# Group A's query and key projected together for three row blocks, and the first loads regrouped

## The chip, the cores and the metric

The kernel runs on one core of one Trainium2 chip. The number that counts is the device time of one execution in microseconds: the median of three executions of the kernel before is 319.23 us (319.03 to 319.84).

## The reference

One decoder layer in float32 over 256 rows of 1024 values, with two groups of attention heads side by side:

```
xn = RMSNorm(x)
[qA|kA|vA|c_q|c_kv|k_rope] = xn @ W_in      # 512, 512, 512, 768, 256, 32 columns
A: 8 heads of 64, dilated windows (128,1),(512,4),(2048,16), QK-norm, bias by distance
B: 8 heads of latent attention: qb = RMSNorm(c_q) @ W_uq, [k|v] = RMSNorm(c_kv) @ W_ukv,
   shared rotary key, QK-norm, dense causal softmax
h   = x + concat(A, B) @ W_o
out = h + relu(RMSNorm(h) @ W1)^2 @ W2
```

## The kernel before, in words

Every product is made of three matmuls in a fast float32 form: each operand is split into a high part (ACT casts it) and a low part (DVE subtracts), and hi·hi, hi·lo and lo·hi are added up in PSUM (`three`, L267). So every weight block passes through ACT (L216, tile `his`) and DVE (L217, tile `los`) before PE may use it, and so does every activation block (L245 on ACT, L246 on DVE, tile `two`). The weights come as one packed array in chunks in the order of use. SP issues the loads in the order of the program text (L206, three buffers `raw`); split pieces have five buffers.

x arrives transposed and unscaled (`xraw`, eight blocks of 128 rows); `split_scaled` multiplies by the norm's gain, which lies in `cols`, a small tile that ACT's own DMA queue loads (L189). The row's own norm factor is applied later. The projections then follow in the order q of group A, k of group A, the latents `cq0`, `cq1` and `kv`, and `va` (the values of group A). Each accumulates over eight row blocks into two banks of the pool `acc` (four banks), one for each half of the 256 rows. q and k are normed, transposed on PE (L375) and written to `qT_a` and `kT_a`; six units of scores, softmax and transposes (`probs`, `keys_first`) follow for group A. The latents wait in `nats`; `transposed_split` (L249) turns them on PE through a bank of the pool `mm` (two banks) and splits them into `cT`, a tile of the pool `two`. From `cT` the up-projections `uq0`, `uq1`, `ukv0`, `ukv1` start, and from there PE's order is written out by hand (`STEPS`, L111).

Ahead of `STEPS` the framework's scheduler sets the order on each engine: it lists the program with a model of the times and writes one fixed order for each engine. Each engine then works through its own list and waits at an instruction until its operands are there and its output buffer is free.

Of the kernel before, what the change touches and what calls it, by code (L numbers as in the profile page):

```python
# [51 lines left out]
def shape_constants():  # L52
# [9 lines left out]
    for i, d in enumerate(dist):  # L62
        if d >= 0:
# [9 lines left out]

G_MIX, G_FFN, G_C, G_QKA, G_QKB, C_ROPE = 0, 8, 16, 24, 26, 28
C_INV = C_ROPE + 2 * ROPE
# [4 lines left out]
CHUNK = 2048  # L80
SOURCE = {"cq0": "w_in", "cq1": "w_in", "kv": "w_in", "qa": "w_in", "ka": "w_in", "va": "w_in", "uq0": "w_uq",
          "uq1": "w_uq", "ukv0": "w_ukv", "ukv1": "w_ukv", "wo": "w_o", "ff1": "w_ff1", "ff2": "w_ff2"}
CHUNKS = [(f"{z}a", 4 * i, 4, c, 512) for z, c in (("q", 0), ("k", 512)) for i in range(2)]
CHUNKS += [(f"cq{b}", 4 * i, 4, CQ0 + 384 * b, 384) for b in range(2) for i in range(2)]
CHUNKS += [("kv", 4 * i, 4, KV0, KVR + ROPE) for i in range(2)]
CHUNKS += [("va", 4 * i, 4, 1024, 512) for i in range(2)]
CHUNKS += [(f"uq{b}", 4 * i, 4 - 2 * i, 384 * b, 384) for b in range(2) for i in range(2)]
CHUNKS += [(f"ukv{b}", 0, 2, 512 * b, 512) for b in range(2)]
CHUNKS += [("wo", 0, 4, 512 * b, 512) for b in range(2)]
CHUNKS += [("wo", 4 + 2 * i, 2, 512 * b, 512) for i in range(2) for b in range(2)]  # L90
_FF1 = [[("ff1", 4 * i, 4, n * FB, FB) for i in range(2)] for n in range(NFB)]
_FF2 = [[("ff2", 4 * n + 2 * i, 2, 0, DM) for i in range(2)] for n in range(NFB)]
CHUNKS += _FF1[0] + sum([_FF1[n] + _FF2[n - 1] for n in range(1, NFB)], []) + _FF2[NFB - 1]
OFFSETS = [0]
for _c in CHUNKS:
    OFFSETS.append(OFFSETS[-1] + P * _c[2] * _c[4])

PIECE = 1024
PIECES = []
for _i, _c in enumerate(CHUNKS):  # L100
    _step = -(-_c[2] // -(-_c[2] * _c[4] // PIECE))
    PIECES += [(_i, _r, min(_step, _c[2] - _r), _c[4]) for _r in range(0, _c[2], _step)]

# [47 lines left out]
def tile_layer(ctx, tc, x, xt, pos_in, cols_in, rows_in, w_all, out):  # L151
# [42 lines left out]
    queue = {"load": 0, "split": 0, "at": 0, "raw": {}, "parts": {}}  # L194

    def load_next(cuts=(0,)):

        i = queue["load"]
        _, _, a, _, n = CHUNKS[i]
        raw = raws.tile([P, CHUNK], F32, name="raw")[:, :a * n]  # L200
        o = OFFSETS[i]
        src = w_all[o:o + P * a * n].rearrange("(p n) -> p n", p=P)
        queue["raw"][i] = raw.rearrange("p (a n) -> p a n", a=a)
        queue["load"] += 1
        for c0, c1 in zip(cuts, cuts[1:] + (a,)):
            nc.sync.dma_start(out=raw[:, c0 * n:c1 * n], in_=src[:, c0 * n:c1 * n])  # L206
            yield

    def split_next():
        i = queue["split"]  # L210
        c, r, a, n = PIECES[i]
        while queue["load"] <= c:
            list(load_next())
        raw = queue["raw"][c][:, r:r + a, :]
        hi, lo = (p.tile([P, PIECE], F32R, name=p.name)[:, :a * n].rearrange("p (a n) -> p a n", a=a) for p in (his, los))
        A.copy(out=hi, in_=raw)  # L216
        V.tensor_tensor(out=lo, in0=raw, in1=hi.bitcast(F32), op=ALU.subtract)  # L217
        queue["parts"][i] = hi, lo
        queue["split"] += 1
# [21 lines left out]
    def gain(i):  # L241
        return cols[:, i:i + 1]

    def split_scaled(src, g, hi, lo):
        a = A.activation(out=hi, in_=src, func=AF.Copy, scale=g)  # L245
        v = V.scalar_tensor_tensor(out=lo, in0=src, scalar=g, in1=hi.bitcast(F32), op0=ALU.mult, op1=ALU.subtract)  # L246
        return a.ins, v.ins
# [51 lines left out]
    starts = [load_next((0, 1, 2, 3)), load_next((0, 2)), load_next((0, 2))]  # L299
    next(starts[0])  # L300
    for k in range(0, KD, 2):
        nc.sync.dma_start(out=xraw[:, k:k + 2, :], in_=xt[k * P:(k + 2) * P, :].rearrange("(k p) s -> p k s", p=P))
        next(starts[k // 4])
        if k == 0:
            split_next()
        elif k == 2:
            next(starts[0])
        for kk in (k, k + 1):
            split_scaled(xraw[:, kk, :], gain(G_MIX + kk), xT[0][:, kk, :], xT[1][:, kk, :])
            if kk == 2:  # L310
                split_next()
        split_next()
    next(starts[2])
    nc.sync.dma_start(out=rows, in_=rows_in)
    nc.sync.dma_start(out=xs[0], in_=x[0:P, :])
    next(starts[2])
    nc.sync.dma_start(out=xs[1], in_=x[P:2 * P, :])
    nc.sync.dma_start(out=pos_i, in_=pos_in)

# [41 lines left out]

    for name in ("qa", "ka"):
        ps = project(name, xT, 0, KD)
        for t in range(NT):
# [201 lines left out]
    qk_b = tiny(1, "qk_b")  # L566
    V.scalar_tensor_tensor(out=qk_b, in0=gain(G_QKB), scalar=-1.0 / math.sqrt(DB), in1=gain(G_QKB + 1), op0=ALU.mult, op1=ALU.mult)
    s_q = [tiny(NT * 4, f"s_q{b}").rearrange("p (t h) -> p t h", t=NT) for b in range(2)]
# [173 lines left out]
def packed_cols(i):  # L742

    rows = [i[n].reshape(-1, P) for n in ("norm_mix_g", "norm_ffn_g", "cq_norm_g", "ckv_norm_g")]
# [3 lines left out]
    return np.concatenate([np.concatenate(rows).T, np.broadcast_to(wide, (P, wide.size))], axis=1)  # L748


# [4 lines left out]
def packed_weights(i):  # L755

    return np.concatenate([i[w][k0 * P:(k0 + a) * P, c0:c0 + n].reshape(a, P, n).transpose(1, 0, 2).reshape(-1)
                           for w, k0, a, c0, n in ((SOURCE[c[0]], *c[1:]) for c in CHUNKS)])

# [20 lines left out]
```

## Time and profile before

| what | value |
|---|---|
| median of three executions | 319.23 us (319.03 to 319.84) |
| the profiled execution | 320.25 us |
| span of its instructions | 318.5 us |
| PE (matmul) busy | 311.1 us, 98% of the span |
| DVE busy | 216.5 us, 68% |
| ACT busy | 176.5 us, 55% |
| POOL busy | 38.4 us, 12% |
| first matmul of a projection | at 6.49 us |

The profiled execution's own time lies 1.75 us above its span, and 1.02 us above the median of the three others. Busy time says how long an engine had an instruction in it; PE's matmuls overlap, so the distance between the starts of two of them is what counts there, not the duration of one.

### The profile page before, as it was taken

Reading aid. Unit: us, or ns where it says so; the run is one execution under the profiler, and the core shown is the slowest. Engines: PE = TensorE matmul, PEld = TensorE weight load, DVE = VectorE, ACT = ScalarE, POOL = GpSimd, SP = SyncE. Lnnn points to the kernel's source line nnn. Section 1 sums busy time; section 2 is a strip of 40 time slices with the busy share of each in tenths; the row PEclk is TensorE's granted clock in tenths of the full one; section 3 lists DMA queues with packets and bytes.
Section 4 is the critical chain, followed back from the end, with each engine's and each line's share of the span. In section 5 each row is a group of like instructions: output and inputs, shape, how many; then the busy total and the mean of one; then the engine's idle time right before and its main releaser. Section 6 shows DMA issues by size and latency. Waiting matters only on the chain.

```text
span 318.5 us, 4481 instructions
## 1 busy us (share of the span) xinstructions
PE 311.1 (98%) x1642; PEld 266.0 (84%) x1642; DVE 216.5 (68%) x416; ACT 176.5 (55%) x314; POOL 38.4 (12%) x61
## 2 busy tenths in 40 slices
PE   6999999999999999999999999999999999999995
PEld 4878999989987887888888888888888888888883
DVE  3869899964887994647896574764755845846622
ACT  4875558957796584429574454444643644545400
POOL 1026501080368000001000000000000000000000
PEclk9999999999999999999999999999999999999999
DMA  7989554243842174305577456646446365553002
GB/s 215 389 336 324 189 188 197 66 151 75 315 141 66 68 262 134 134 0 206 191 255 273 163 204 182 241 138 224 173 150 245 137 227 182 176 205 132 0 31 103
DMA packets 12294, 56.43 MB, mean 177 GB/s; under 512 B 1480, under 2 KB 3792, under 8 KB 7536
## 3 DMA queue, kind: packets, MB, share of 16 engines
q1 hardware_dynamic: 11072, 55.02, 49.7%
q10 hardware_dynamic: 1200, 1.12, 1.1%
q8 instruction: 13, 0.21, 0.2%
q14 instruction: 9, 0.07, 0.1%
HBM read 55.07 MB, written 1.06 MB: 176 GB/s over the span
## 4 chain that ended last, share of the span: by engine, by line
PE 96%; DMA 1%; ACT 1%; DVE 0%; issue 0%; DVEq 0%; SPq 0%; ACTq 0%
PE acc L144 57%; PE sc L144 20%; PE mm L144 15%; PE mm L147 4%; DMA big<-in_xt_dram 1%; ACT big L576 0%; ACT sqs L359 0%; ACT two L245 0%; ACT nats L596 0%; DVE x L723 0%; DVEq L776 0%; SPq L206 0%; ACT vb L600 0%; ACTq L245 0%
## 5 line engine op out<-in xcount | busy, mean ns | idle before, releaser
L217 DVE TENSOR_TENSOR los<-raw,his 128x1024 fp32r<-128x1024 f32 (+3 forms) x106 | 121.3, 1150 | 68.9 <-ACT his L216 68.7
L216 ACT CAST his<-raw 128x1024 fp32r<-128x1024 f32 (+3 forms) x106 | 104.1, 992 | 89.8 <-PE acc L144 41.9
L144 PE MATMUL acc<-his,two 128*128 128x512 f32 (+2 forms) x320 | 96.3, 375 | 1.5 <-ACT two L245 1.5
L144 PEld LDWEIGHTS acc<-his,two 128*128 128x128 f32 x320 | 59.4, 191 | 9.5 <-ACT two L245 2.3
L144 PE MATMUL acc<-two,his 128*128 128x512 f32 x240 | 63.2, 393 | 0.0
L144 PE MATMUL acc<-los,two 128*128 128x512 f32 (+2 forms) x160 | 59.6, 373 | 0.0
L144 PE MATMUL sc<-his,big 128*128 128x512 f32 x128 | 49.0, 389 | 0.0
L144 PE MATMUL mm<-his,big 128*128 128x512 f32 x128 | 49.0, 389 | 0.0
L144 PEld LDWEIGHTS acc<-two,his 128*128 128x128 f32 x240 | 42.6, 189 | 7.1
L144 PEld LDWEIGHTS acc<-two,los 128*128 128x128 f32 x240 | 34.5, 190 | 3.4
L144 PE MATMUL acc<-two,los 128*128 128x256 f32 x240 | 35.8, 282 | 0.0
L144 PEld LDWEIGHTS acc<-los,two 128*128 128x128 f32 x160 | 30.6, 192 | 3.9 <-issue 0.6
L144 PEld LDWEIGHTS mm<-his,big 128*128 128x128 f32 x128 | 24.0, 188 | 5.1
L144 PEld LDWEIGHTS sc<-his,big 128*128 128x128 f32 x128 | 24.1, 188 | 4.8
L144 PE MATMUL sc<-los,big 128*128 128x512 f32 x64 | 25.0, 390 | 0.0
L144 PE MATMUL mm<-los,big 128*128 128x512 f32 x64 | 24.9, 389 | 0.0
L408 ACT ACTIVATE half<-half,mx 128x128 f32<-128x128 f32 (+1 forms) x32 | 14.2, 445 | 4.4 <-DVE mx L405 4.3
L144 PEld LDWEIGHTS mm<-los,big 128*128 128x128 f32 x64 | 12.0, 188 | 2.5
L694 ACT COPY half<-acc 128x256 f32<-128x256 f32 x30 | 9.7, 372 | 7.8 <-PE acc L144 7.8
L144 PEld LDWEIGHTS sc<-los,big 128*128 128x128 f32 x64 | 12.0, 188 | 2.2
L695 DVE TENSOR_TENSOR half<-acc,half 128x256 f32<-128x256 f32 x30 | 11.3, 416 | 1.3 <-ACT half L694 1.3
L246 DVE SCALAR_TENSOR_TENSOR two<-mm,cols,two 128x256 fp32r<-128x256 f32 x16 | 7.3, 481 | 6.5 <-ACT two L245 6.3
(140 smaller groups left out, 282.9 us busy)
## 6 DMA issues: line engine op xcount, KB each, us to landing
raw<-in_weights_dram SPq DMA_DIRECT2D x37, 1024.0 KB, 4.8
raw<-in_weights_dram SPq DMA_DIRECT2D x10, 512.0 KB, 3.7
raw<-in_weights_dram SPq DMA_DIRECT2D x6, 768.0 KB, 4.3
raw<-in_weights_dram SPq DMA_DIRECT2D x2, 576.0 KB, 4.1
raw<-in_weights_dram SPq DMA_DIRECT2D x4, 256.0 KB, 5.7
big<-in_xt_dram SPq DMA_DIRECT2D x4, 256.0 KB, 5.7
x<-in_x_dram SPq DMA_DIRECT2D x2, 512.0 KB, 8.3
big<-vec_d ACTq DMA_DIRECT2D x1, 1024.0 KB, 6.8
```

The source lines that it names most:

```text
L144: return self._issue(self.tc.nc.tensor.matmul(**kw))
L147: return self._issue(self.tc.nc.tensor.transpose(**kw))
L216: A.copy(out=hi, in_=raw)
L217: V.tensor_tensor(out=lo, in0=raw, in1=hi.bitcast(F32), op=ALU.subtract)
L246: v = V.scalar_tensor_tensor(out=lo, in0=src, scalar=g, in1=hi.bitcast(F32), op0=ALU.mult, op1=ALU.subtract)
L408: A.activation(out=sb[:, i, :], in_=sb[:, i, :], func=AF.Exp, scale=-1.0, bias=mx[:, i:i + 1], accum_out=mx[:, 4 + i:5 + i])
L694: A.copy(out=zs, in_=ps[2 * b + i][:, S:])
L695: V.tensor_tensor(out=zs, in0=ps[2 * b + i][:, 0:S], in1=zs, op=ALU.add)
```

## The change

The weights of q and k of group A become one sequence `qk` of sixteen blocks of 128 rows by 512 columns: for the row blocks 0, 1 and 2 the q block and then the k block, after that q for the blocks 3 to 7 and k for the blocks 3 to 7. Both products accumulate at the same time, in all four banks of `acc`. The transposed x is packed by partition on the host, with the gains of the first norm in front of it; ACT's queue loads the gains and x block 0 in one DMA (`first`), and SP loads block 1 alone and the others in pairs. All loads and splits of this opening are kept in program order. `cols` (without those gains), `rows` and `pos_i` are loaded after the last chunk of `qk`, and the two products of gains `qk_a` and `qk_b` move from DVE (one instruction each) to POOL (two each).

```diff
+TOGETHER = 3
+QK = [(k, z) for k in range(TOGETHER) for z in range(2)] + [(k, z) for z in range(2) for k in range(TOGETHER, KD)]
...
+CHUNKS = [("qk", [(k, 512 * z) for k, z in QK[4 * i:4 * i + 4]], 512) for i in range(4)]
...
+    first = const.tile([P, NMIX + S], F32, name="first")
+    A.dma_start(out=first, in_=xt[:, 0:NMIX + S])
...
-    A.dma_start(out=cols, in_=cols_in)
...
+    def pinned(ins):
+        return tc.keep_in_program_order(ins) if starting else ins
...
+    starts = [load_next(cuts) for cuts in ((0, 1, 2), (0, 2), (0, 2), (0, 2))]
+    for chunk_or_x in (0, (1, 2), 0, 0, (2, 4), 1, (4, 6), 1, (6, 8), 2, 2):
+        if isinstance(chunk_or_x, int):
+            next(starts[chunk_or_x])
+        else:
+            load_x(*chunk_or_x)
+    split_x(0)
+    split_next()
+    split_next()
+    for k in range(1, KD):
+        split_x(k)
+        if k in (1, 2, 4, 6, 7):
             split_next()
+        if k == 1:
+            split_next()
+    load(out=xs[0], in_=x[0:P, :])
+    load(out=xs[1], in_=x[P:2 * P, :])
+    next(starts[3])
+    next(starts[3])
+    load(out=cols, in_=cols_in)
+    load(out=rows, in_=rows_in)
+    load(out=pos_i, in_=pos_in)
+    starting.clear()
...
-    V.scalar_tensor_tensor(out=qk_a, in0=gain(G_QKA), scalar=1.0 / math.sqrt(DA), in1=gain(G_QKA + 1), op0=ALU.mult, op1=ALU.mult)
+    G.tensor_tensor(out=qk_a, in0=gain(G_QKA), in1=gain(G_QKA + 1), op=ALU.mult)
+    G.tensor_scalar(out=qk_a, in0=qk_a, scalar1=1.0 / math.sqrt(DA), scalar2=None, op0=ALU.mult)
...
+    qk_ps = [[bank(acc) for _ in range(NT)] for _ in range(2)]
+    def qk_steps():
+        i = 0
+        while i < len(QK):
+            w = weights("qk")
+            for j in range(w[0].shape[1]):
+                k, z = QK[i]
+                three(qk_ps[z], xT, w, k, j, k == 0, k == KD - 1)
+                i += 1
+                yield k, z
```

The order on the engines moves with it, also far behind the edited lines, since the scheduler writes it anew. On PE, the first matmuls behind the four warming ones; `acc_218` and `acc_219` are q's two banks before:

```order
L144 MATMUL sc_121<-half_102 128x256 x4
L144 MATMUL acc_218<-his_131,two_126 128x512
L144 MATMUL acc_218<-los_132,two_126 128x512
L144 MATMUL acc_219<-his_131,two_126 128x512
L144 MATMUL acc_219<-los_132,two_126 128x512
L144 MATMUL acc_218<-his_131,two_126 128x512
L144 MATMUL acc_219<-his_131,two_126 128x512
```

The same place now; `acc_231` and `acc_232` are q's banks, `acc_233` and `acc_234` k's, `his_144` and `his_148` the high parts of the first q and the first k block:

```order
L155 MATMUL sc_122<-half_102 128x256 x4
L155 MATMUL acc_231<-his_144,two_127 128x512
L155 MATMUL acc_232<-his_144,two_127 128x512
L155 MATMUL acc_233<-his_148,two_127 128x512
L155 MATMUL acc_234<-his_148,two_127 128x512
L155 MATMUL acc_231<-los_145,two_127 128x512
L155 MATMUL acc_231<-his_144,two_127 128x512
```

The first two matmuls are followed by two of k's, which need the second weight block; before, six matmuls stood on the first block alone.

On PE, the end of the value projection and the begin of `uq0`, before; `mm_603` holds the transposes of the latents' blocks 0 and 1, `mm_612` that of block 2, `acc_878` and `acc_879` are the banks of `va`, `acc_963` is the first of `uq0`. Fourteen matmuls of `va` lie between the two groups of transposes:

```order
L147 MATMUL mm_603<-ident_114,nats_521 128x128
L147 MATMUL mm_603<-ident_114,nats_522 128x128
L147 MATMUL mm_603<-ident_114,nats_521 128x128
L147 MATMUL mm_603<-ident_114,nats_522 128x128
L144 MATMUL acc_879<-los_917,two_126 128x512
L144 MATMUL acc_879<-his_916,two_126 128x512
...
L144 MATMUL acc_879<-his_932,two_126 128x512
L144 MATMUL acc_879<-los_933,two_126 128x512
L144 MATMUL acc_879<-his_932,two_126 128x512
L147 MATMUL mm_612<-ident_114,nats_521 128x128
L147 MATMUL mm_612<-ident_114,nats_522 128x128
L144 MATMUL acc_963<-his_967,two_525 128x384
```

The same place now, with `mm_606` and `mm_615` for those transposes, `acc_881` and `acc_882` for `va` and `acc_967` for `uq0`:

```order
L155 MATMUL acc_882<-los_936,two_127 128x512
L155 MATMUL acc_882<-his_935,two_127 128x512
L158 MATMUL mm_606<-ident_115,nats_524 128x128
L158 MATMUL mm_606<-ident_115,nats_525 128x128
L158 MATMUL mm_606<-ident_115,nats_524 128x128
L158 MATMUL mm_606<-ident_115,nats_525 128x128
L158 MATMUL mm_615<-ident_115,nats_524 128x128
L158 MATMUL mm_615<-ident_115,nats_525 128x128
L155 MATMUL acc_967<-his_971,two_528 128x384
L155 MATMUL acc_967<-los_972,two_528 128x384
L155 MATMUL acc_967<-his_971,two_528 128x384
L155 MATMUL acc_968<-his_971,two_528 128x384
```

The four transposes of `mm_606` have moved behind the last matmul of `va`, straight ahead of the products that read their splits.

On ACT in the same place, before; `two_525` is the tile of `cT`, written from the transposes' banks, `va0` and `va1` the results of the value projection:

```order
L245 ACTIVATE two_525<-mm_603,cols_108 128x256
L216 CAST his_1042<-raw_1040 128x768
L245 ACTIVATE two_525<-mm_603,cols_108 128x256
L560 ACTIVATE va0_211<-acc_878,rstd_192 128x512
L560 ACTIVATE va1_212<-acc_879,rstd_192 128x512
L216 CAST his_1058<-raw_1040 128x768
L245 ACTIVATE two_525<-mm_612,cols_108 128x256
L245 ACTIVATE two_525<-mm_693,cols_108 128x256
L216 CAST his_1076<-raw_1074 128x768
```

And now; `two_528` is the tile of `cT`:

```order
L476 COPY pts_399<-mm_500 128x2x256
L239 CAST his_1046<-raw_1044 128x768
L476 COPY pts_399<-mm_518 128x2x256
L610 ACTIVATE va0_223<-acc_881,rstd_204 128x512
L610 ACTIVATE va1_224<-acc_882,rstd_204 128x512
L239 CAST his_1062<-raw_1044 128x768
L268 ACTIVATE two_528<-mm_606,cols_110 128x256
L268 ACTIVATE two_528<-mm_615,cols_110 128x256
L268 ACTIVATE two_528<-mm_606,cols_110 128x256
```

Both splits from the first bank have moved from ahead of `va0` to behind `va0`, `va1` and the cast of a weight piece. DVE's list has the low halves in the same order, behind the low half of that weight piece.

## Rows read from the trace of the kernel before

**Rows 1.** Section 1 of the page: busy time, share of the span, instructions

```profile
PE 311.1 (98%) x1642; PEld 266.0 (84%) x1642; DVE 216.5 (68%) x416; ACT 176.5 (55%) x314; POOL 38.4 (12%) x61
```

**Rows 2.** The waits of PE in the whole span: total, times, longest

```profile
PE acc L144 <- ACT two L245: 1.5, 1, 1.5
...
PE mm L147 <- ACT sqs L359: 0.5, 1, 0.5
```

**Rows 3.** Windows: stretch, length, busy time per engine, clock, DMA share, GB/s

```profile
4.00:6.49 2.49, 0.96 (x4) 0.24 (x2) 0.94 (x4) 1.18 (x3) 0.00 (x0) 1.00 0.98 308
6.49:10.50 4.01, 4.01 (x10) 3.14 (x11) 3.72 (x8) 3.69 (x8) 0.00 (x0) 1.00 1.05 398
31.00:60.00 29.00, 29.00 (x185) 28.28 (x185) 26.49 (x93) 20.15 (x52) 5.88 (x8) 1.00 0.49 172
60.00:90.00 30.00, 30.00 (x173) 27.57 (x172) 21.85 (x48) 21.68 (x46) 11.38 (x21) 1.00 0.51 173
```

**Rows 4.** The first matmuls: start, duration, operation, idle before and releaser

```profile
4.32 0.63 PE L144 MATMUL sc<-half 128*128 128x256 f32 x1
6.49 0.79 PE L144 MATMUL acc<-his,two 128*128 128x512 f32 x1 [1.53 <-ACT two L245]
...
8.36 1.91 PE L144 MATMUL acc<-his,two 128*128 128x512 f32 x4
10.07 0.63 PE L144 MATMUL acc<-los,two 128*128 128x512 f32 x1
```

**Rows 5.** ACT at the start: the first splits

```profile
5.13 0.62 ACT L216 CAST his<-raw 128x512 fp32r<-128x512 f32 x1 [2.46 <-DMA raw<-in_weights_dram]
5.93 0.91 ACT L245 ACTIVATE two<-big,cols 128x256 fp32r<-128x256 f32 x2 [0.18 <-DMA big<-in_xt_dram]
7.00 0.62 ACT L216 CAST his<-raw 128x512 fp32r<-128x512 f32 x1 [0.16 <-DMA raw<-in_weights_dram]
```

**Rows 6.** DMA issues by line: KB each, median us to landing

```profile
raw<-in_weights_dram SPq DMA_DIRECT2D x4, 256.0 KB, 5.7
...
cols<-in_cols_dram ACTq DMA_DIRECT2D x1, 54.0 KB, 4.5
```

**Rows 7.** PE at the end of the value projection

```profile
75.01 0.39 PE L144 MATMUL acc<-los,two 128*128 128x512 f32 x1
75.24 0.39 PE L144 MATMUL acc<-his,two 128*128 128x512 f32 x1
75.47 0.38 PE L147 MATMUL mm<-ident,nats 128*128 128x128 f32 x2
75.61 0.42 PE L144 MATMUL acc<-his,two 128*128 128x384 f32 x1
...
76.04 0.52 PE L144 MATMUL acc<-his,two 128*128 128x384 f32 x2
```

**Rows 8.** ACT in the same stretch

```profile
72.52 0.48 ACT L245 ACTIVATE two<-mm,cols 128x256 fp32r<-128x256 f32 x1
...
74.99 1.38 ACT L560 ACTIVATE va<-acc,rstd 128x512 f32<-128x512 f32 x2 [0.84 <-PE acc L144]
76.25 0.82 ACT L216 CAST his<-raw 128x768 fp32r<-128x768 f32 x1
76.98 0.47 ACT L245 ACTIVATE two<-mm,cols 128x256 fp32r<-128x256 f32 x1
```

**Rows 9.** DVE in the same stretch

```profile
77.11 0.96 DVE L217 TENSOR_TENSOR los<-raw,his 128x768 fp32r<-128x768 f32 x1 [1.95 <-ACT his L216]
77.99 0.87 DVE L246 SCALAR_TENSOR_TENSOR two<-mm,cols,two 128x256 fp32r<-128x256 f32 x2
```

**Rows 10.** Last group A probabilities on DVE, the transposes behind on PE

```profile
66.07 0.61 DVE L411 TENSOR_SCALAR half<-half,mx 128x256 f32<-128x256 f32 x2
...
71.41 0.60 PE L147 MATMUL mm<-ident,half 128*128 128x128 f32 x4
71.84 0.60 PE L147 MATMUL mm<-ident,nats 128*128 128x128 f32 x4
```

More of the change, by code (lines that the diff above doesn't have):

```diff
@@ L80 @@
 CHUNK = 2048
-SOURCE = {"cq0": "w_in", "cq1": "w_in", "kv": "w_in", "qa": "w_in", "ka": "w_in", "va": "w_in", "uq0": "w_uq",
+SOURCE = {"cq0": "w_in", "cq1": "w_in", "kv": "w_in", "qk": "w_in", "va": "w_in", "uq0": "w_uq",
           "uq1": "w_uq", "ukv0": "w_ukv", "ukv1": "w_ukv", "wo": "w_o", "ff1": "w_ff1", "ff2": "w_ff2"}
-CHUNKS = [(f"{z}a", 4 * i, 4, c, 512) for z, c in (("q", 0), ("k", 512)) for i in range(2)]
-CHUNKS += [(f"cq{b}", 4 * i, 4, CQ0 + 384 * b, 384) for b in range(2) for i in range(2)]
@@ L85 @@
[L85 to L91, printed above, removed]
@@ L92, with chunk @@
-_FF2 = [[("ff2", 4 * n + 2 * i, 2, 0, DM) for i in range(2)] for n in range(NFB)]
+TOGETHER = 3
+QK = [(k, z) for k in range(TOGETHER) for z in range(2)] + [(k, z) for z in range(2) for k in range(TOGETHER, KD)]
+def chunk(name, k0, a, c0, n):
+    return name, [(k0 + i, c0) for i in range(a)], n
+CHUNKS = [("qk", [(k, 512 * z) for k, z in QK[4 * i:4 * i + 4]], 512) for i in range(4)]
+CHUNKS += [chunk(f"cq{b}", 4 * i, 4, CQ0 + 384 * b, 384) for b in range(2) for i in range(2)]
+CHUNKS += [chunk("kv", 4 * i, 4, KV0, KVR + ROPE) for i in range(2)]
@@ new lines @@
+CHUNKS += [chunk("va", 4 * i, 4, 1024, 512) for i in range(2)]
+CHUNKS += [chunk(f"uq{b}", 4 * i, 4 - 2 * i, 384 * b, 384) for b in range(2) for i in range(2)]
+CHUNKS += [chunk(f"ukv{b}", 0, 2, 512 * b, 512) for b in range(2)]
+CHUNKS += [chunk("wo", 0, 4, 512 * b, 512) for b in range(2)]
+CHUNKS += [chunk("wo", 4 + 2 * i, 2, 512 * b, 512) for i in range(2) for b in range(2)]
+_FF1 = [[chunk("ff1", 4 * i, 4, n * FB, FB) for i in range(2)] for n in range(NFB)]
+_FF2 = [[chunk("ff2", 4 * n + 2 * i, 2, 0, DM) for i in range(2)] for n in range(NFB)]
@@ L93 @@
 CHUNKS += _FF1[0] + sum([_FF1[n] + _FF2[n - 1] for n in range(1, NFB)], []) + _FF2[NFB - 1]
 OFFSETS = [0]
-for _c in CHUNKS:
-    OFFSETS.append(OFFSETS[-1] + P * _c[2] * _c[4])
+for _, _b, _n in CHUNKS:
+    OFFSETS.append(OFFSETS[-1] + P * len(_b) * _n)
 PIECE = 1024
 PIECES = []
-for _i, _c in enumerate(CHUNKS):
-    _step = -(-_c[2] // -(-_c[2] * _c[4] // PIECE))
-    PIECES += [(_i, _r, min(_step, _c[2] - _r), _c[4]) for _r in range(0, _c[2], _step)]
+for _i, (_, _b, _n) in enumerate(CHUNKS):
+    _a = len(_b)
+    _step = -(-_a // -(-_a * _n // PIECE))
+    PIECES += [(_i, _r, min(_step, _a - _r), _n) for _r in range(0, _a, _step)]
@@ L194, in tile_layer, with load @@
     queue = {"load": 0, "split": 0, "at": 0, "raw": {}, "parts": {}}
+    starting = [True]
+    def pinned(ins):
+        return tc.keep_in_program_order(ins) if starting else ins
+    def load(**kw):
+        pinned(nc.sync.dma_start(**kw))
     def load_next(cuts=(0,)):
         i = queue["load"]
-        _, _, a, _, n = CHUNKS[i]
+        _, blocks, n = CHUNKS[i]
+        a = len(blocks)
         raw = raws.tile([P, CHUNK], F32, name="raw")[:, :a * n]
@@ L205, in load_next @@
         for c0, c1 in zip(cuts, cuts[1:] + (a,)):
-            nc.sync.dma_start(out=raw[:, c0 * n:c1 * n], in_=src[:, c0 * n:c1 * n])
+            load(out=raw[:, c0 * n:c1 * n], in_=src[:, c0 * n:c1 * n])
             yield
@@ L298, in tile_layer, with load_x, split_x @@
     xT = pair()
[L299 to L304, printed above, removed]
-            split_next()
[L306 to L318, printed above, removed]
+    def load_x(k0, k1):
+        load(out=xraw[:, k0:k1, :], in_=xt[:, NMIX + k0 * S:NMIX + k1 * S].rearrange("p (k s) -> p k s", s=S))
+    def split_x(k):
+        src = xraw[:, k, :] if k else first[:, NMIX:]
+        split_scaled(src, first[:, k:k + 1], xT[0][:, k, :], xT[1][:, k, :])
+    starts = [load_next(cuts) for cuts in ((0, 1, 2), (0, 2), (0, 2), (0, 2))]
[10 more added lines that the diff above has]
+        if k in (1, 2, 4, 6, 7):
+            split_next()
+        if k == 1:
[8 more added lines that the diff above has]
+    starting.clear()
     def sumsq(src, dst):
@@ L360, in head_sums @@
         V.tensor_reduce(out=dst, in_=sqv, op=ALU.add, axis=AX.X)
-    for name in ("qa", "ka"):
-        ps = project(name, xT, 0, KD)
+    qk_ps = [[bank(acc) for _ in range(NT)] for _ in range(2)]
[8 more added lines that the diff above has]
+                yield k, z
+    steps = qk_steps()
+    for z, name in enumerate(("qa", "ka")):
+        while next(steps) != (KD - 1, z):
+            pass
+        ps = qk_ps[z]
         for t in range(NT):
@@ L742, in packed_cols @@
 def packed_cols(i):
-    rows = [i[n].reshape(-1, P) for n in ("norm_mix_g", "norm_ffn_g", "cq_norm_g", "ckv_norm_g")]
+    rows = [i[n].reshape(-1, P) for n in ("norm_ffn_g", "cq_norm_g", "ckv_norm_g")]
     rows += [np.tile(i[n], 2)[None] for n in ("qnorm_a_g", "knorm_a_g")]
@@ L755, in packed_weights @@
 def packed_weights(i):
-    return np.concatenate([i[w][k0 * P:(k0 + a) * P, c0:c0 + n].reshape(a, P, n).transpose(1, 0, 2).reshape(-1)
-                           for w, k0, a, c0, n in ((SOURCE[c[0]], *c[1:]) for c in CHUNKS)])
+    return np.concatenate([np.stack([i[SOURCE[name]][k * P:(k + 1) * P, c:c + n] for k, c in blocks], axis=1).reshape(-1)
+                           for name, blocks, n in CHUNKS])
 def kernel(**inputs):
@@ L766 @@
     x = i["x"][0]
-    laid = {"x": x, "xt": x.T, "positions": i["positions"].reshape(NT, P).T, "cols": packed_cols(i),
+    laid = {"x": x, "xt": packed_x(x, i["norm_mix_g"]), "positions": i["positions"].reshape(NT, P).T, "cols": packed_cols(i),
             "rows": packed_rows(i), "weights": packed_weights(i)}
```

16 lines of the change are left out of this document (10 added, 6 removed).

## The prediction

> **What bounds the kernel now.** I read the page's busy shares first: PE has 98% of the span [rows 1], so the question is where PE stands still and whether the change touches that. The list of PE's waits comes next. It holds a wait of 1.5 us for ACT ahead of the first projection and one of 0.5 us much later [rows 2]; nothing else of weight is left. The windows say the same by stretch: from 31 to 60 and from 60 to 90 us PE is busy for all 29.0 and all 30.0 us, while DVE has 26.49 of the 29 [rows 3]. There is next to no stall to win behind the start, and each new wait of PE is paid in full: nothing later has slack to give it back. So only two kinds of places count: the opening, and places where the new order makes PE wait.
>
> The opening costs PE two things. The first projection matmul starts at 6.49, after 1.53 us of idleness behind the warming matmuls [rows 4]. And it runs at half pace: from 8.36 to 10.07 there are four matmuls of 512 columns, 0.427 us each, against 0.23 us from 75.01 to 75.24 [rows 4, 7]; 512 columns in 0.427 us are the 1.2 GHz level, 0.23 us is near the 2.4 GHz one. The windows' clock column reads 1.00 even at 4.00 to 6.49 [rows 3], so here the pace of the matmuls tells the level.
>
> **The opening, part by part.** Before, the start hangs on ACT: the cast of the first weight block begins when it lands (5.13, 0.62 us), then x is split (two blocks in 0.91 us from 5.93), and PE starts 0.1 us after the first of these [rows 4, 5]. Now ACT's queue brings the gains and x block 0 (132 KB) in place of `cols` (54 KB), and SP brings the same first weight block. `cols` took 4.5 us, so it landed at about 5.2 beside the weight block at 5.1 [rows 5, 6]. The extra 78 KB cost 0.25 us at the 308 GB/s of that stretch [rows 3]. Both at 5.35 or so, then x (0.46) and the cast (0.62), then 0.1: start at about 6.5, no gain. The bounds: if x lands first and its split hides in the wait for the weights, the start is 5.13 + 0.62 + 0.1 = 5.85 (0.64 us gained); if `first`, with its 128 separate pieces, takes as long as a block of 256 KB did (5.7 us [rows 6], so 6.4), the start is 7.6 (1.1 us lost). No row shows such a load; I take 6.45, by the nearest row, that of `cols`.
>
> The Trainium skill (DMA: Bandwidth & Descriptors, "Anatomy of one DMA — SWDGE (gpsimd) path") fits a DMA as about 2.0 us plus bytes over 436 GB/s. By it, 388 KB issued at once would be there in 2.9 us. The trace disagrees already before the change: 54 KB took 4.5 us [rows 6], so I give that only a rival's chance.
>
> PE's third matmul now needs the cast of a second weight block. Before, the second block began its cast at 7.00 [rows 5] with about 0.5 MB of loads ahead of it, as now; its cast ends at 7.65. PE comes there at 6.45 + 0.59 + 0.43 = 7.5: a wait of 0.2 us. Further on nothing is short: each row block now brings twelve matmuls, 2.7 us even at full pace, for 640 KB, which take 1.6 us at the 398 GB/s of the windows [rows 3]. The opening sums to +0.15 us.
>
> What else moves there is covered. The two gain products leave DVE (0.15 us each) and become four short operations on POOL, which is 12% busy [rows 1]. `cols`, `rows` and `pos_i` land near 20 us (6.1 MB at that rate behind the first block at 5.1); their first readers on PE and POOL come behind 24 us, when q is complete. Cover gone, PE's bias product would stand in the way until `rows` lands. The later norms of q (complete after 66 matmuls of the pair, not 48 of q alone) have the 30 remaining k matmuls, 6.8 us, as cover, where they had 48; PE waited for none of them before [rows 2].
>
> **The end of the value projection.** Here the order moves against PE. Before, the transposes of latent blocks 0 and 1 stand at 71.84 among the matmuls of `va` [rows 10], and ACT splits block 0 at 72.52, 3 us before `uq0` reads it at 75.61 [rows 7, 8]. Now these transposes come behind the last matmul of `va`, and on ACT the split of block 0 stands behind two evacuations of `va` and a cast of weights, exactly the place that block 2's split has before. So its times can be read off. Call S the start of the last `va` matmul, 75.24 before. ACT evacuates `va` from 74.99 on (1.38 us, bound by the end of the matmuls), casts at 76.25 and splits at 76.98, until 77.45: S + 2.2 [rows 8]. On DVE, the low half of the cast piece runs at 77.11 and the first split's low half from 77.99, done about 78.45: S + 3.2 [rows 9]. PE itself would be ready early: one matmul (0.23) and six transposes (0.6) behind S, at S + 0.85.
>
> - `uq0`'s first matmul waits for the high half until S + 2.25: 1.4 us.
> - Its third needs the low half. It would be due 0.43 us after the first (75.61 to 76.04 [rows 7]), at S + 2.7, and gets it at S + 3.3: 0.6 us.
> - The next transposes need the bank whose second low half comes 0.8 us after the first; the four matmuls between take 0.7: under 0.1 us.
>
> That is 2.05 us. Cross-check: `uq0`'s third matmul stands at 76.04 before; four transposes (0.43, from 71.41 to 71.84 [rows 10]) now come after S, so S lies at 74.8 and the third matmul at 78.1, 2.06 later. The lower bound is the wait for the high half alone, 1.4 us, if DVE is not held by the weight piece; the upper 2.3, if the first evacuation starts late. The later orders on PE and ACT are again those of before, so the delay stays.
>
> **The sum.** +0.15 + 2.05 = +2.2 us. From the profiled execution, 320.25 us (318.5 of span and 1.75 around it), that is 322.45; the profiled execution lies 1.02 above the median of 319.23, and from the median it is **321.4 us**.
>
> **Rivals.**
> - *The new order doesn't bind* (about 319.3, no change): the splits would have to reach PE in time. For it: before, no such wait shows in the same region. Against: the split cannot begin before its transposes end, and those stand behind `va`; only ACT's list could be quicker than its rows. 0.12.
> - *The early loads win* (faster): if 388 KB land by 3.6 us, x and the cast are done at 4.7, and PE goes on when its last warming matmul ends at 4.95 [rows 4], 1.54 us sooner. Without the pause the rise to full pace could come before the projection has run 4.0 us at half of it; that stretch costs 4.0 x (1 - 0.227/0.427) = 1.9 us. Together up to 3.4, minus 2.05: 317.9. It decides from a start before about 5.0. This is the outcome of the fit above. 0.06.
> - *The new wait drops the clock* (slower still): the wait of 1.4 us is nearly as long as the pause of 1.53, after which PE ran at half pace [rows 4]. Another half-paced stretch of 4.0 us adds 1.9: 323.3. The Trainium skill (TensorE: Matmul & The Clock Gate, "The HAM clock gate") says that idleness brings the half rate back. Against: before that pause the clock had not risen, so no row shows a fall. 0.07.
> - *The softmax comes late on DVE* (slower): the rotary tables start later, and some 1.5 us of their small operations now fall among group A's probabilities, where DVE has 26.49 of 29 us [rows 3]. The last probabilities were ready at 66.68, their transposes due at 71.41 [rows 10]: 4.7 us of room. Against: three times the 1.5. If an earlier unit with less room is 1.2 us late: 322.6. 0.09.
>
> **How the numbers follow.** The forecast has 0.66. About what a measurement can tell here from no change is 0.3%, 0.96 us; the forecast's own range, 1.4 - 0.6 to 2.3 + 1.1 us over the median, is 320.0 to 322.6, so nearly all of it is slower: 0.64, with the clock and softmax rivals 0.80. No change gets 0.02 + 0.10 + 0.01 = 0.13; faster 0.02 + 0.05 = 0.07. The range reaches down past the rival without change, to 319.1, and up to 322.8: under it lie half of that rival and the early loads (0.12), above it the fallen clock and a little more (0.08).
>
> **What would show it.** Right: one wait of PE for the ACT split of the latents of about 1.4 us near 75, another of 0.6 us for DVE's low half within 1 us of it, and the first matmul between 6.2 and 6.8 with a wait of some 0.2 us at the third. Wrong: no wait near 75; a first matmul before 5.5 or after 7; matmuls of 0.63 us behind the new wait; or waits of PE between 30 and 72 us for probabilities.

## The result, and the profile after

| what | before | after |
|---|---|---|
| median of the four executions timed side by side | 319.53 us (319.03 to 319.84) | 323.21 us (321.92 to 323.63) |
| ratio, with its 95% interval | | 1.0102 (1.0080 to 1.0124) |
| the profiled execution, and its span | 320.25 us, 318.5 us | 323.22 us, 321.4 us |
| mean granted clock of TensorE in it | 0.999 | 0.994 |

The changed kernel is slower: by 3.7 us between these medians, where the forecast was 2.2. The 323.21 lies 0.4 us above the range's upper end; the ratio, applied to the earlier median, gives 319.23 x 1.0102 = 322.5, which lies inside. A second set of twelve executions (the fifth experiment) gave 322.26 us and 1.0074 (1.0049 to 1.0100): their spread, 319.88 to 323.73, is itself part of the answer.

The busy times of the page say little, as before [rows 1]: PE has 2.5 us more, in the same 1642 instructions.

```profile
PE 313.6 (98%) x1642; PEld 267.4 (83%) x1642; DVE 215.5 (67%) x414; ACT 176.5 (55%) x314; POOL 39.5 (12%) x65
```

The waits of PE (total, times, longest) tell more. The opening's 1.5 us for `two` [rows 2] has become 0.5 us for a weight cast; two new waits stand beside the old one of half a microsecond.

```profile
PE acc L155 <- ACT two L268: 1.2, 1, 1.2
...
PE mm L158 <- ACT sqs L393: 0.6, 1, 0.6
PE acc L155 <- ACT his L239: 0.5, 1, 0.5
PE acc L155 <- DVE two L269: 0.4, 1, 0.4
```

The windows of [rows 3] again: from 31 to 60 PE is still busy throughout; from 60 to 90 it lacks 1.6 us, and the clock column, 1.00 before, reads 0.94.

```profile
31.00:60.00 29.00, 29.00 (x189) 28.59 (x188) 27.54 (x97) 20.42 (x50) 5.99 (x9) 1.00 0.62 211
60.00:90.00 30.00, 28.39 (x150) 25.32 (x150) 19.06 (x46) 19.36 (x43) 8.79 (x21) 0.94 0.46 149
```

**The opening.** On ACT (start, duration, operation, idle before), x block 0 is split at 4.36, so `first`, issued at 0.72, landed within 3.6 us, and the first weight block was there when that split ended: its cast starts at 4.77, without a wait, against 5.13 before [rows 5].

```profile
4.36 0.51 ACT L268 ACTIVATE two<-first 128x256 fp32r<-128x256 f32 x1 [1.68 <-DMA first<-in_xt_dram]
4.77 0.60 ACT L239 CAST his<-raw 128x512 fp32r<-128x512 f32 x1
5.90 0.62 ACT L239 CAST his<-raw 128x512 fp32r<-128x512 f32 x1 [0.53 <-DMA raw<-in_weights_dram]
```

PE starts at 5.42 (6.49 before [rows 4]) and works at half pace until 10.15, where the duration of one matmul falls from 0.63 to 0.40:

```profile
5.42 2.37 PE L155 MATMUL acc<-his,two 128*128 128x512 f32 x4 [0.47 <-ACT his L239]
...
9.30 0.63 PE L155 MATMUL acc<-los,two 128*128 128x512 f32 x1
...
10.15 0.40 PE L155 MATMUL acc<-los,two 128*128 128x512 f32 x1
```

The 0.47 us ahead of 5.42 is PE's idleness in front of the first projection matmul (the warming matmuls end at 4.95). The four matmuls of that row start at 5.42, 6.02, 6.57 and 7.16; at half pace the third, which needs the second weight block, is 0.13 us late.

I call the loss of a stretch what PE loses there against the usual distance of matmuls of the same shape at full pace (0.228 us for 512 columns), summed over all matmul starts of the trace. Up to 20 us it is 5.9 us before and 5.0 after: a gain of 0.9.

**The end of the value projection.** PE, ACT and DVE stand as the order said they would. The last `va` matmul starts at 74.17; the six transposes follow, then PE stands idle twice:

```profile
74.17 0.39 PE L155 MATMUL acc<-his,two 128*128 128x512 f32 x1
74.40 0.82 PE L158 MATMUL mm<-ident,nats 128*128 128x128 f32 x6
76.44 0.44 PE L155 MATMUL acc<-his,two 128*128 128x384 f32 x1 [1.22 <-ACT two L268]
76.72 0.34 PE L155 MATMUL acc<-los,two 128*128 128x384 f32 x1
77.45 0.61 PE L155 MATMUL acc<-his,two 128*128 128x384 f32 x2 [0.39 <-DVE two L269]
...
80.66 0.52 PE L155 MATMUL acc<-los,two 128*128 128x384 f32 x1
80.98 0.84 PE L155 MATMUL acc<-his,two 128*128 128x384 f32 x2
...
82.23 0.33 PE L155 MATMUL acc<-los,two 128*128 128x384 f32 x1
82.41 0.51 PE L155 MATMUL acc<-his,two 128*128 128x384 f32 x2
```

ACT in the same stretch, with the two evacuations and the cast ahead of the splits, where before block 2's split stood behind them [rows 8]:

```profile
73.90 1.38 ACT L610 ACTIVATE va<-acc,rstd 128x512 f32<-128x512 f32 x2 [0.57 <-PE acc L155]
75.18 0.82 ACT L239 CAST his<-raw 128x768 fp32r<-128x768 f32 x1
75.91 0.84 ACT L268 ACTIVATE two<-mm,cols 128x256 fp32r<-128x256 f32 x2
```

And DVE, where the weight piece still stands ahead of the low halves [rows 9]:

```profile
76.04 0.96 DVE L240 TENSOR_TENSOR los<-raw,his 128x768 fp32r<-128x768 f32 x1 [2.79 <-ACT his L239]
76.91 0.87 DVE L269 SCALAR_TENSOR_TENSOR two<-mm,cols,two 128x256 fp32r<-128x256 f32 x2
```

The idle times printed (1.22 and 0.39) leave out the modelled tails of the matmuls; from start to start PE loses 1.38 and 0.56 us, 1.94 in all. Behind them comes a loss that the waits don't show. Matmuls of 384 columns stand 0.32 us apart (80.66 to 80.98), and from 82.23 on 0.18 again. Windows cut at these points give the clock; the granted clock is 0.50 of full speed, the 1.2 GHz level, for 3.4 us:

```profile
75.00:78.40 3.40, 1.79 (x10) 1.22 (x9) 2.21 (x4) 2.22 (x5) 0.00 (x0) 1.00 0.18 27
78.40:81.80 3.40, 3.40 (x15) 3.30 (x13) 1.38 (x4) 1.58 (x4) 0.00 (x0) 0.50 0.35 130
81.80:85.20 3.40, 3.40 (x23) 3.37 (x22) 1.22 (x2) 1.91 (x3) 0.00 (x0) 1.00 0.29 41
```

PE is busy in all of the 3.40 us and does 15 matmuls where the next 3.40 us hold 23: half pace for 3.4 us costs 1.7. So the spans nearly balance: 1.9 of waits and 1.7 to 1.8 of half pace, minus 0.9 in the opening, make 2.7 to 2.8 of the 2.9 us between 318.5 and 321.4. The medians differ by 3.7 because the profiled execution of before was 0.7 above its median.

### The profile page after: what moved, and what is told of

The parts are those of the page before. It is cut to its first block, busy times and chain, and to the rows that moved or that the text cites. A ratio compares the mean times of both kernels' runs of the same rounds, so it can differ in the third digit from the quotient of the medians.

```text
span 321.4 us, 4485 instructions
## 1 busy us (share of the span) xinstructions
PE 313.6 (98%) x1642; PEld 267.4 (83%) x1642; DVE 215.5 (67%) x414; ACT 176.5 (55%) x314; POOL 39.5 (12%) x65
## 4 chain that ended last, share of the span: by engine, by line
PE 95%; ACT 2%; DMA 1%; DVE 1%; issue 0%; DVEq 0%
PE acc L155 57%; PE sc L155 20%; PE mm L155 14%; PE mm L158 4%; DMA first<-in_xt_dram 1%; ACT va L610 0%; ACT big L627 0%; ACT his L239 0%; DVE los L240 0%; ACT sqs L393 0%; ACT nats L647 0%; ACT two L268 0%; DVE x L774 0%; DVE two L269 0%; DVEq L832 0%
## 5 line engine op out<-in xcount | busy, mean ns | idle before, releaser
L155 PE MATMUL acc<-his,two 128*128 128x512 f32 (+2 forms) x320 | 98.3, 380 | 2.1 <-ACT two L268 1.2
L268 ACT ACTIVATE two<-mm,cols 128x256 fp32r<-128x256 f32 x16 | 7.3, 477 | 9.3 <-PE mm L158 8.4
```

The source lines that it names most:

```text
L155: return self._issue(self.tc.nc.tensor.matmul(**kw))
L268: a = pinned(A.activation(out=hi, in_=src, func=AF.Copy, scale=g))
```

## The experiments

The theory was: waits at `uq0`, which come from the order alone, and the fall of the clock behind them, minus a faster opening. The rivals: the pairing and the moved loads cost the time, or the fall has another cause. The sets (experiments 1 to 4, 5 to 8, 9 to 11) ran on three chips, and the changed kernel was run again only in the second. In every set the kernel before ran on the same chip, with medians of 319.77 to 319.80; a comparison across sets rests on that agreement.

Since the pace differs between executions, I also count those with a mean granted clock of 0.995 or less. A fall of 3.4 us takes 0.5 x 3.4 / 321 = 0.0053 off the mean. The end of an execution takes up to 0.003 more: in the profile above PE is done at 317.56 and the granted clock is 0.50 again from 320.75 to the end at 321.4, which takes another 0.001. The thirteen profiles agree with the count: the one with a fall in its middle reads 0.994, the others 0.997 to 1.000; no execution of any set reads 0.996. Of the kernel before, 9 of 80 executions read 0.995 or less.

**1. The transposes put ahead again.** The last twelve `va` matmuls are ordered behind the fourth transpose:

```diff
-    ps = project("va", xT, 0, KD)
+    ps = []
+    va_steps = project_steps("va", xT, 0, KD, ps.extend)
+    for _ in range(6):
+        next(va_steps)
+    with tc.issue_after(turned[3]):
+        list(va_steps)
```

> The changed kernel, with PE's last twelve matmuls of the value projection (row blocks 6 and 7) put behind the transposes of latent blocks 0 and 1, so that ACT splits these blocks ahead of va0 and va1 as the kernel before does. Theory (the loss sits at uq0's first matmuls: 1.9 us of waits for the splits and some 1.8 us of half pace behind them, and the opening gained 0.9): no wait of PE near 75 us, matmuls of 384 columns at 0.17 us all along, and the time 0.9 us under the kernel before, about 318.4 to 318.7. Rival A (the paired projection and the moved loads cost the time, the wait at uq0 only shows it): still 2 us or more above the kernel before. Rival B (the clock falls near 78 us without the wait): about 1 us above the kernel before, with matmuls 0.32 us apart near 78.

Median 318.89 (317.71 to 320.63), ratio 0.9981 (0.9961 to 1.0001): 0.9 under the kernel before, as the theory had it, though 0.2 above its range, and the interval just includes no change. No wait is left between the transposes and `uq0`, and 384 columns take 0.18 us:

```profile
73.25 0.38 PE L158 MATMUL mm<-ident,nats 128*128 128x128 f32 x2
73.39 0.42 PE L155 MATMUL acc<-his,two 128*128 128x384 f32 x1
73.64 0.34 PE L155 MATMUL acc<-los,two 128*128 128x384 f32 x1
73.82 0.52 PE L155 MATMUL acc<-his,two 128*128 128x384 f32 x2
```

Rivals A and B fall here. But the opening, unedited, is not that of the profile above: PE reaches full pace over 3 us earlier.

```profile
5.41 1.60 PE L155 MATMUL acc<-his,two 128*128 128x512 f32 x4 [0.46 <-ACT his L239]
6.85 0.39 PE L155 MATMUL acc<-los,two 128*128 128x512 f32 x1
```

**2. The late split in the kernel before.** Its opening is left alone:

```diff
 STEPS:
-"q0*6 ...
+"q0 x q0*5 ...
 latents:
-        transposed_split([c[:, b * 384:] for c in cn], 3 * b, 3, G_C, *cT[:2])
...
-    transposed_split([c[:, QR:] for c in cn], KQ, KKV, G_C, *cT[:2])
 behind va's evacuations:
+    transposed_split([c[:, 0:] for c in cn], 0, 3, G_C, *cT[:2])
 step "x":
+        transposed_split([c[:, 384:] for c in cn], 3, 3, G_C, *cT[:2])
+        transposed_split([c[:, QR:] for c in cn], KQ, KKV, G_C, *cT[:2])
```

> The kernel before, its opening untouched, with the transposes of the latent blocks written behind the value projection: PE's and ACT's lists at uq0 then read as in the changed kernel (ACT: va0, va1, a weight cast, then the split of block 0). Theory: PE waits 1.2 to 1.4 us for ACT and 0.4 to 0.6 us for DVE at uq0's first and third matmul, and runs 384 columns at 0.32 us for about 3 us behind that: the kernel before plus 3.5 to 3.9 us. Rival A (pairing and loads cost the time): within 0.5 us of the kernel before. Rival B (the fall of the clock comes from something else in the changed kernel): plus 1.9 us, no slow matmuls behind the wait.

Median 324.15 (322.55 to 326.30), ratio 1.0147 (1.0111 to 1.0182). The two waits came out as in the changed kernel, and a third that I had not expected: the ten transposes that now stand together need a bank that DVE frees late.

```profile
76.52 0.44 PE L144 MATMUL acc<-his,two 128*128 128x384 f32 x1 [1.22 <-ACT two L245]
...
77.53 0.62 PE L144 MATMUL acc<-his,two 128*128 128x384 f32 x2 [0.40 <-DVE two L246]
...
80.43 0.65 PE L147 MATMUL mm<-ident,nats 128*128 128x128 f32 x4 [1.26 <-DVE two L246]
```

Rival A falls: without pairing and moved loads the order alone costs 4.4 us. Of these, 1.4 (from start to start) are the third wait, which the changed kernel does not have. On the clock it is split: in the profiled execution (323.28) there is no fall in spite of 3.36 us of waits, while three of the six have a mean clock of 0.989, twice the drop of one fall, and take 325.02 to 326.30. A fall goes with waits, but not in each execution.

**3. The waits filled.** Ten matmuls stand ahead of `uq0`'s first matmul, four ahead of its third:

```diff
+    fill_ps = bank(sc)
+    def fill(n):
+        for _ in range(n):
+            T.matmul(out=fill_ps[:, 0:S], lhsT=xT[0][:, 0, 0:P], rhs=xT[0][:, 0, :], start=True, stop=True)
...
+    with tc.issue_after(turned[5]):
+        fill(10)
+    between.append(lambda: fill(4))
```

> The changed kernel with idle PE time at uq0 filled: ten matmuls of 256 columns (about 0.115 us each) into an unused bank between the transposes and uq0's first matmul, and four more ahead of its third. Their results are read by nobody; the waits for ACT and DVE stay as long as they were, but PE works in them. Theory (the idleness of the two waits makes the clock fall): uq0's first matmul no earlier than in the changed kernel, but no slow matmuls behind it; 1.8 us under the changed kernel, thus 1.1 to 1.9 us above the kernel before. Rival B (the clock falls for another reason): the same time as the changed kernel, matmuls 0.32 us apart near 79.

Median 320.45 (319.95 to 323.68), ratio 1.0039 (1.0023 to 1.0055): 2.8 under the changed kernel's first set, 1.8 under its second, and one execution of twelve at 0.995 or less. It is 0.7 above the kernel before, less than the 1.1 to 1.9 expected. Nothing got earlier. In the profile the last `va` matmul stands at 76.15, `uq0`'s first 2.27 us and its third 3.28 us behind it, as in the changed kernel (2.27 and 3.28):

```profile
76.15 0.39 PE L155 MATMUL acc<-his,two 128*128 128x512 f32 x1
...
76.95 1.43 PE L155 MATMUL sc<-two 128*128 128x256 f32 x10
78.42 0.44 PE L155 MATMUL acc<-his,two 128*128 128x384 f32 x1
...
78.87 0.63 PE L155 MATMUL sc<-two 128*128 128x256 f32 x4
79.43 0.62 PE L155 MATMUL acc<-his,two 128*128 128x384 f32 x2
```

So, by the counts (1 of 12 here, 12 of 16 in the changed kernel, see the fifth experiment), idleness makes the clock fall, and work that nobody needs holds it. (The profiled execution is this set's longest, 323.68: its opening is still at half pace after 12 us.)

**4. No pairing.**

```diff
-TOGETHER = 3
+TOGETHER = 0
```

> The changed kernel with no row block paired (q for all eight row blocks, then k), the new load of the gains with x block 0, the new order of the loads and the pinned splits all kept. In its order the transposes of latent blocks 0 and 1 stand among the value projection's matmuls again, as in the kernel before. Theory (the gain of the opening comes from the small first load, the loss from the order at uq0): first matmul near 5.4, no wait at uq0: 0.5 to 0.9 us under the kernel before. Rival A (the regrouped loads cost the time): above the kernel before by 2 us. Rival C (the gain of the opening needs the pairing, because q alone runs out of weights): PE waits of about 0.9 us for casts in the opening, the time within 0.3 us of the kernel before.

Median 319.81 (319.51 to 320.04), ratio 1.0004 (0.9994 to 1.0014). The theory's gain did not come; rival C had it. PE starts at 5.39 and reaches full pace near 7, and then there is nothing for it to do: it waits for x.

```profile
5.39 1.22 PE L155 MATMUL acc<-his,two 128*128 128x512 f32 x2 [0.44 <-ACT his L239]
...
9.65 0.50 PE L155 MATMUL acc<-his,two 128*128 128x512 f32 x1 [0.55 <-ACT two L268]
```

In this profile, with six matmuls per row block, the loads set the opening; that would be why these executions differ by 0.5 us only. With twelve PE sets it, and its clock shows in the time.

**5. The changed kernel again.**

> The changed kernel as it is, in more executions and with a second profile. The profiles of the first four experiments show that PE's rise to full pace in the opening comes at 5.1 to 13.5 us, differently from one execution to the next, also where the opening is the same code; and their executions spread over 0.5 to 3.7 us. Theory (at uq0 the waits of 1.9 us are in every execution, the fall of the clock behind them in nearly every one; the pace of the opening varies): median 322.5 to 323.5, a spread of 1.5 to 3 us, uq0's two waits again 1.4 and 0.6 us, and slow matmuls behind them. Rival (the fall was a chance of one profile): executions near 321 with a mean clock of 0.998 or more, and no slow matmuls in this profile.

Median 322.26 (319.88 to 323.73). Eight of twelve are at 0.995 or less, with the first set 12 of 16 (the 13 in the expectations of the ninth experiment is a miscount). The profile caught one without a fall, 319.88. Its waits are the same 1.38 and 0.55 us, its opening is fast:

```profile
5.33 1.86 PE L155 MATMUL acc<-his,two 128*128 128x512 f32 x4 [0.38 <-ACT his L239]
7.04 0.39 PE L155 MATMUL acc<-los,two 128*128 128x512 f32 x1
...
74.69 0.45 PE L155 MATMUL acc<-his,two 128*128 128x384 f32 x1 [1.22 <-ACT two L268]
...
75.70 0.61 PE L155 MATMUL acc<-his,two 128*128 128x384 f32 x2 [0.39 <-DVE two L269]
...
78.91 0.33 PE L155 MATMUL acc<-los,two 128*128 128x384 f32 x1
79.08 0.51 PE L155 MATMUL acc<-his,two 128*128 128x384 f32 x2
```

Two profiles of one program are 3.3 us apart, and the parts are known: 1.7 for the fall, and 1.7 for the opening (a loss of 3.3 up to 20 us here, 5.0 there). The theory is right on the waits. It missed the rest: the median lies below its 322.5 to 323.5, the spread of 3.85 us above its 3, and a fall in 8 of 12 is not "nearly every one"; the profile, without slow matmuls, is the one that the rival had described. Still, with 8 of 12 the fall was no chance of one profile.

**6. One cast behind.** Only ACT's cast for `uq1` moves (entry 2 is the split of latent block 2, the second in ACT's list):

```diff
+        with ExitStack() as after:
+            if CHUNKS[c][0] == "uq1" and (CHUNKS[c][1][0][0], r) == (0, 2):
+                after.enter_context(tc.issue_after(latent_splits[2]))
-        pinned(A.copy(out=hi, in_=raw))
+            pinned(A.copy(out=hi, in_=raw))
```

> The changed kernel with one instruction of ACT moved: the cast of a weight piece of uq1 that stands between va1's evacuation and the split of latent block 0 comes behind the first two splits. PE's list is that of the changed kernel. Theory (the wait is the sum of what stands ahead of the split on ACT, and the length of the wait decides about the clock): the wait at uq0's first matmul shrinks by the cast, 0.73 us, to some 0.65, that at the third to 0.2 or less; if the clock then stays up, the time is 1.1 + 1.8 = 2.9 us under the changed kernel, about the kernel before plus 0.5; if it falls all the same, 1.1 us under the changed kernel. Rival (the wait is bound by the transposes or by va's evacuations, not by the cast): no change against the changed kernel.

Median 320.43 (319.12 to 322.44), ratio 1.0025 (1.0003 to 1.0047): 1.8 under the changed kernel beside it, between the two figures. The wait shrank to 0.65 us from start to start, as forecast, and 0.2 us of idleness appeared a little later; two of twelve are at 0.995 or less.

```profile
74.29 0.44 PE L155 MATMUL acc<-his,two 128*128 128x384 f32 x1 [0.49 <-ACT two L271]
...
76.77 0.44 PE L158 MATMUL mm<-ident,nats 128*128 128x128 f32 x2 [0.20 <-DVE two L272]
```

The rival falls: the queue ahead of the split on ACT is the wait.

**7 and 8. q's matmuls first, and a fifth warming matmul.** To the first experiment, k's first block is ordered behind q's; then a fifth warming matmul is added:

```diff
+                with ExitStack() as after:
+                    if i == 1:
+                        after.enter_context(tc.issue_after(q_done))
-                three(qk_ps[z], xT, w, k, j, k == 0, k == KD - 1)
+                    q_done = three(qk_ps[z], xT, w, k, j, k == 0, k == KD - 1)
...
-WARM = 4
+WARM = 5
```

> As the first experiment (transposes ahead of the last matmuls of the value projection), and in the opening PE's six matmuls of q on row block 0 stand ahead of the six of k, so that the third matmul no longer needs the cast of the second weight block. Theory: the opening's wait of 0.47 us at the third matmul goes, the first matmul stays at 5.4: 0.3 to 0.5 us under the first experiment, 1.0 to 1.4 under the kernel before. Rival (the wait only moves to the low half of the first block or to k's first matmul, or the varying pace of the opening hides it): within 0.3 us of the first experiment.

> As the seventh experiment, with a fifth warming matmul (0.43 us) that fills PE's idle time between the fourth (ends at 4.95) and the first projection matmul (5.4). Theory (the late rise of the clock in some executions comes from PE's idleness ahead of the projection): the first matmul stays within 0.1 us, the rise comes earlier in more of the executions, the spread shrinks to the lower end of the first experiment's (317.7 to 318.5), and the median falls by 0.5 us or more against the seventh. Rival (the time of the rise is not set by that pause): the same median and spread as the seventh.

The seventh: 318.17 (317.76 to 319.18), ratio 0.9952 (0.9937 to 0.9967), 0.7 under the first experiment's median, which stands in another set. The eighth: 318.10 (317.82 to 318.49), 0.9948 (0.9929 to 0.9967). Both beat the kernel before by 1.6 to 1.7 us and are the fastest here. The wait of 0.47 us that the seventh's expectation places at the third matmul stands, in the profiles, ahead of the first, and the edit did not touch it; in the seventh's profile it is 0.83, because the warming matmuls reached full pace from about 4.1 us on and were done sooner. Where full pace comes that early, the third matmul does wait for k's cast without the edit: in the sixth's profile it starts at 6.59, 0.54 us late, and in the seventh's at 6.15, with q's low part in place of k's high part:

```profile
5.42 0.73 PE L155 MATMUL acc<-his,two 128*128 128x512 f32 x2 [0.83 <-ACT his L239]
6.15 0.50 PE L155 MATMUL acc<-los,two 128*128 128x512 f32 x1
```

So the edit can save some 0.4 us in such executions; that it made the 0.7 is not shown. The shortest executions are alike (317.71 in the first experiment, 317.76 here), and what is missing here are the long ones (above 319.2, six of twelve there, none of nine here).

The fifth warming matmul (two passes of 0.43 us, at 4.75 and 5.17) closes the pause: the first product starts at 5.45 without idleness. It gives nothing more: rival right. Whether it narrows the spread, six executions can't tell.

**9 and 10. Each wait filled alone.** Against the third experiment:

```diff
 9:
-    between.append(lambda: fill(4))
 10:
-        fill(10)
```

> As the third experiment, with the ten matmuls of 256 columns in the first wait at uq0 (for ACT) alone; the second, 0.56 us for DVE's low half, stays idle. The executions so far: mean clock 0.995 or less (which is what an execution with a fall shows) in 13 of 16 of the changed kernel, in 1 of 12 with both waits filled. Theory (the long first wait is what makes the clock fall): 0 to 3 of 12 executions at 0.995 or less, no slow matmuls behind uq0, median within 0.4 us of the third experiment's 320.45. Rival (any wait there does it, or both together): 8 or more of 12, median near the changed kernel's 322.3.

> The counterpart: four matmuls of 256 columns in the second wait (for DVE's low half) alone; the first, 1.38 us for ACT, stays idle. Theory (the first wait is what makes the clock fall): 7 to 10 of 12 executions at a mean clock of 0.995 or less, median 321.9 to 322.8. Rival (it takes both waits together): 0 to 4 of 12, median near 320.5.

With the first filled, 1 of 8 executions is at 0.995 or less; with the second filled, none of 12, though PE stands idle for the same 1.38 us ahead of `uq0`:

```profile
75.35 0.44 PE L155 MATMUL acc<-his,two 128*128 128x384 f32 x1 [1.22 <-ACT two L268]
...
75.81 0.63 PE L155 MATMUL sc<-two 128*128 128x256 f32 x4
```

My theory (the long wait alone) falls, the rival is right: it takes both, 1.38 and 0.56 us with two matmuls between them, or as much idleness as their sum; no run separates these two. The medians, 321.88 and 320.99, miss both forecasts: seven of the ninth's eight are at 321.68 to 322.17, and its profile shows one of these, without a fall and with an opening at half pace until 10.

**11. One block paired,** the rest as the seventh:

```diff
-TOGETHER = 3
+TOGETHER = 1
```

> As the seventh experiment (order at uq0 repaired, q's six matmuls on row block 0 ahead of k's), with one row block paired instead of three. Without pairing (fourth experiment) the time was that of the kernel before, with waits of 0.55 us for x and 0.4 us for casts in the opening; with three paired it was 1.6 us lower. Theory (pairing gives PE twelve matmuls per row block where the loads bring less than PE could use at full pace): between the two, 318.4 to 319.4, with a wait of PE of 0.3 to 0.6 us for row block 2 or 3 in the profile. Rival (the gain comes from the earlier first matmul and the repaired order, and the first pair is enough): 318.0 to 318.4, no such wait.

Median 318.62 (318.19 to 319.75), ratio 0.9972 (0.9956 to 0.9988): 0.4 above three blocks (in another set, beside the same time of the kernel before) and 1.2 under none, where two other edits differ as well. The time is in the theory's range, the wait that I named is not in the profile, whose opening ran at half pace until 10. That the number of pairs makes the difference is therefore not shown.

## Why the prediction was right on the waits, and off in size

- **PE is the bound and pays each wait in full**: right. The losses behind 90 us are those of before.
- **The new waits at `uq0`, 1.4 + 0.6 + under 0.1 = 2.05 us**: right. From the last `va` matmul (74.17) the steps gave 76.42 for the first matmul and 77.47 for the third; they stand at 76.44 and 77.45, 1.94 us of loss, and nothing further. That the queue on ACT makes them was shown by taking one cast (sixth) or both splits (first) out of it, and by putting them into the kernel before (second).
- **The opening, +0.15 us**: mis-sized, and of the wrong sign. I took `first` to need what `cols` did, 4.5 us; it took 3.6 or less, and the weight block was there by 4.77 instead of 5.13. So PE started at 5.42, outside my bounds (5.85 to 7.6) and before the 5.5 that I had named as a sign of being wrong. The wait at the third matmul, 0.2, came out at 0.13. The gain was 0.9 us in the profile, and 0.9 in the medians of the first experiment. And I took the half-paced stretch for a fixed price; with the pairing it is what differs most between executions. That the early start is worth something only together with twelve matmuls per row block (0.9 us in the first experiment, nothing in the fourth, neither with a wait at `uq0`) I had not seen: I weighed the loads, and not what PE could do with an early rise.
- **The rival that the new wait drops the clock, 0.07**: it came true on top of the forecast, in 12 of 16 executions, 1.7 us each (I gave it 1.9). This is the step that made the number too low: "no row shows a fall" was taken as a reason against. That reading was wrong too. The trace of before has a fall at its very end (rows below); what no row showed is a fall behind pauses as short as these. The Trainium skill (TensorE: Matmul & The Clock Gate, "The HAM clock gate") says that idleness brings the half rate back, and that the point of the rise differs from run to run; the trace agrees with both (falls behind the waits; full pace from about 6.2 or 10.1 in the same program), though the half a microsecond that the page gives for the second is less than the 3.9 us between these two profiles. Which pauses are enough had to be measured here.
- **The rival of the late softmax**: did not come; PE is busy in all of the 29.00 us from 31 to 60. **The early loads** came in part: x was in use at 4.36 and the weight block at 4.77, not both by 3.6 (the fit quoted there is of loads that POOL issues, these are issued by ACT and SP); so the start was at 5.42, not before 5.0, and the waits outweighed the gain.

The end of the trace of before, in windows: PE is done at 314.53, and the granted clock, the column behind the five engines, is 0.50 from 317.90 on.

```profile
314.50:317.90 3.40, 0.03 (x1) 0.00 (x0) 0.88 (x2) 0.00 (x0) 0.00 (x0) 1.00 0.22 77
317.90:318.46 0.56, 0.00 (x0) 0.00 (x0) 0.00 (x0) 0.00 (x0) 0.00 (x0) 0.50 0.00 0
```

Together: +1.94 + 0.75 x 1.7 - 0.9 = 2.3 us is what an average execution should lose, and the second set shows 2.5 of medians. The first set, where all four had the fall, shows 3.7, while the same sum with a fall in each gives 2.7. Part of the rest may be that the 0.9 is counted from a profiled execution of before that lies 0.7 above its median; with four executions it stays open. The forecast of 2.2 came near the second set by two errors that cancel: an opening 1.05 us too slow and a missing fall worth 1.3 on average. That is luck; the 2.05 for the waits is not.

Open: why the rise in the opening comes at such different points (from about 4.1 to 13.5 us in the thirteen profiles); why it takes both waits, or their sum, for a fall; and where the falls lie in those executions of the kernel before and of the first experiment (3 of 12) that have a mean clock of 0.995 or less, since no profile caught one.

## What to carry to other kernels

When an edit far ahead lets a scheduler rewrite the order, read each engine's list at every hand-over between stages: here one split that fell behind two evacuations and a cast cost more than the edited place could gain, and one ordering constraint gave it back. On an engine that is always busy, count a cluster of new pauses at the price of the pauses and of a stretch at half clock behind them, with a chance that only a dozen executions show. An earlier start pays only where the engine, and not the loads, sets the pace behind it; more work per loaded block brought that about here. Then the clock of the opening starts to matter, so compare distributions, not two profiles.

## What the runs showed of the hardware that was not expected

- The same program reaches full pace at different points: in the two profiles of the changed kernel near 10.1 and 6.2 us, which is 1.7 us of loss in the opening.
- Two waits of 1.38 and 0.56 us, two matmuls apart, went with a fall of the clock in 12 of 16 executions; the first alone in 0 of 12, the second alone in 1 of 8, both filled in 1 of 12. In the profile the fall came 0.9 us after PE had gone on working, and lasted 3.4 us.
- A load of 132 KB, issued at 0.72 us beside the first weight block, was in use at 4.36; one of 54 KB took 4.5 us before.
